# Half-array products of two heads issued in turn, and part of the mixer's VectorE work given to ScalarE, in a two-block transformer kernel on one core

## The chip, the cores and the metric

The kernel runs on one core of one Trainium2 chip. The metric is the device time of one execution in microseconds (us). The profiled execution is a single one, taken by the hardware profiler; its rows are what the prediction is worked out from.

The engines are named as in the profile: PE is TensorE's matrix product, PEld its weight load, DVE is VectorE, ACT is ScalarE, POOL is GpSimd, SP issues most DMAs.

## The reference

Two blocks follow each other on 512 tokens of width 1024 (batch 1). What matters here:

```python
# block 1: a mixer, then cross attention, then a mixture of 32 experts
def one_block(args):                                   # differential attention, 4 heads, 2 halves of 64
    s = jnp.einsum('bhmqd,bhmkd->bhmqk', q_blk, k)     # m = 0, 1: two halves of a head
    p = jax.nn.softmax(jnp.where(causal, s, -jnp.inf), axis=-1)
    a = p[:, :, 0] - lam * p[:, :, 1]
    return jnp.einsum('bhqk,bhkd->bhqd', a.astype(v.dtype), v)
...
qk = jax.nn.silu(causal_depthwise_conv(jnp.concatenate([mq, mk], axis=-1), ml_conv_w, ml_conv_b))  # 4 taps
...
# block 2, twice (two layers): a convolution beside an attention over selected keys
s_raw = jnp.einsum("bthd,bsd->bths", qi_b, k_idx_f)    # 8 index heads of 64
score = jnp.einsum("bth,bths->bts", w_b, jax.nn.relu(s_raw))
_, sel = lax.top_k(score, k_top)                       # 128 keys of each query
probs = jax.nn.softmax(...)                            # 8 heads, over the selected keys
o = jnp.einsum("bthk,btkc->bthc", probs, kv_sel)
o = jnp.einsum("bshc,hcd->bshd", o, w_uv)              # 64 output columns a head
```

The kernel multiplies the latent values by `w_uv` first, so that a head's last product has 64 output rows.

## The kernel before, in words

The program is one core's list of instructions. A scheduler orders them engine by engine, by priorities and its own estimate of times; each engine then works through its list in order. So an instruction that waits holds back what stands behind it on its engine.

Most products are made of float16 halves: a number is split into a high and a low part, and a product is three matrix products that add up in one PSUM bank (`mm3`, line 110: high by high, high by low, low by high; `mm`, line 99, issues each). `split` (lines 128 and 129) makes the parts, the high one on ACT, the low one on DVE. PSUM has eight banks; `bank(tag)` hands out those of a tag in turn. In the mixer `at` has three banks and `tr` two; in the layers of block 2 `at` has two, `tr` two and `po` one.

The changed places, in order of time:

- **Scores of the mixer's attention** (`diff_head`, lines 499 to 526). For each of 4 heads and 4 query blocks i the keys are W = 128 (i + 1) wide. Each half m of a head has 64 channels, so that its `mm3` fills 64 of the array's 128 rows, half 0 the upper and half 1 the lower ones. Then come a mask product (128 rows), on DVE the negated maximum (line 511) and its scaling (512), on ACT the exponential (514); when both halves are there, on DVE a reciprocal (517), a product with lambda (518), the scaling of half 1 (519) and the combination (520).
- **Convolution of the mixer** (`mlstm`, lines 594 to 606), 8 blocks of 128 channels: ACT copies the projection to `u` (595), DVE makes the first tap (597) and three more (600), ACT and DVE finish it. Its projections and those of the mixer's values are ordered between the attention's products.
- **Scores of the index heads** (`select`, line 1597), in each of two layers for query blocks i = 1, 2, 3: 8 heads of 64 channels, even heads in the upper and odd ones in the lower 64 rows. Each head's `mm3` goes to an `at` bank, ACT makes the positive part (1610) into one of two `re` buffers, DVE adds it up with the query's weight (1613, 1615), and then 16 rounds of a maximum and a replacement (1619, 1620) on DVE select the keys.
- **Values of the selected attention** (`dsa`, line 1625), four pairs of heads (hp) in each layer: softmax of a head, transposes by PE to `tr`, `split` into `pT`, and a `mm3` with 64 output rows into the upper (hh = 0) or lower (hh = 1) half of the one `po` bank, for key blocks k = 0 to 3 with 512, 384, 256 and 128 columns. The `pT{k}` have one buffer each.

The gates and the convolution's products of block 2 (`cv`, `mm`) stand between these in PE's list.

Of the kernel before, what the change touches and what calls it, by code (L numbers as in the profile page):

```python
# [12 lines left out]
F16 = mybir.dt.float16  # L13
BF16 = mybir.dt.bfloat16
I32 = mybir.dt.int32
AF = mybir.ActivationFunctionType
OP = mybir.AluOpType
AX = mybir.AxisListType
PSUM = bass.MemoryType.PSUM

P = 128
D = 1024
S = 512
NT = S // P
# [39 lines left out]
class Kern:  # L64
# [44 lines left out]
    def mm3(self, out, L, R, start, stop):  # L109
        self.mm(out, L[0], R[0], start, False)  # L110
        self.mm(out, L[0], R[1], False, False)
        return self.mm(out, L[1], R[0], False, stop)

# [377 lines left out]
    def diff_head(self, low, pool, qkh, qkl, vh, vl, lam, yy, h):  # L491
        nc = self.nc
        sc = 1.0 / (SA * SA * 8.0)
        if True:
# [4 lines left out]
            for i in range(NT):  # L499
# [3 lines left out]
                p = []  # L503
                for m in range(2):
                    rows = slice(m * 64, m * 64 + 64)
                    pS = self.bank("at")
                    qs = [t[rows, h, i * P:(i + 1) * P] for t in (qkh, qkl)]
                    ks = [t[rows, 4 + h, :W] for t in (qkh, qkl)]
                    self.mm3(pS[:, :W], qs, ks, True, False)
                    self.mm(pS[:, i * P:W], self.identb, self.mask_q, False, True)  # L510
                    nc.vector.tensor_reduce(nm[:, m:m + 1], pS[:, :W], AX.X, OP.max, negate=True)
                    nc.vector.tensor_scalar(nm[:, m:m + 1], nm[:, m:m + 1], sc, None, op0=OP.mult)
# [6 lines left out]
                nc.vector.tensor_scalar(p[1][:, :W], p[1][:, :W], sm[:, 1:2], None, op0=OP.mult)  # L519
# [30 lines left out]
    def mlstm(self, pool, xh, xl, qh, ql, gateb, yy):  # L550
# [37 lines left out]
        for k in range(4):  # L588
            w = self.load_w(a["w_pre"][6 + k])
            for bb in range(2):  # L590
# [6 lines left out]
                nc.vector.tensor_scalar(acc, u[:, 3:], convw[:, blk, 3:4], convb[:, blk:blk + 1],  # L597
                                        op0=OP.mult, op1=OP.add)
# [999 lines left out]
    def select(self, pool, i, qih, qil, kih, kil, widx):  # L1598
# [5 lines left out]
        for h in range(8):  # L1604
            rows = slice((h % 2) * 64, (h % 2) * 64 + 64)
            ps = self.bank("at")
            self.mm3(ps[:, :W], (qih[rows, h // 2, t], qil[rows, h // 2, t]),
                     (kih[rows, :W], kil[rows, :W]), True, True)
# [16 lines left out]
    def dsa(self, pool, ga, uq, cqh, cql, kvh, kvl, vh, vl, msk, yh, yl, hp):  # L1625
        nc, a = self.nc, self.a
        sc = 1.0 / (SA * SA * math.sqrt(128.0))
        po = self.bank("po")
        for hh in range(2):
# [26 lines left out]
            f = slice(h * 64, h * 64 + 64)  # L1656
            for k in range(NT):
                n = S - k * P
                pt = self.bank("tr")
                for i in range(k, NT):  # L1660
                    nc.tensor.transpose(pt[:, (i - k) * P:(i - k + 1) * P], ps_[i][:, k * P:(k + 1) * P],  # L1661
                                        self.ident)
                pT = pool.tile([P, 2, n], F16, name="pT", tag=f"pT{k}", bufs=1)
                self.split(pt[:, :n], pT[:, 0], pT[:, 1], 1024.0)
                self.mm3(po[hh * 64:hh * 64 + 64, k * P:], (vh[:, k, f], vl[:, k, f]), (pT[:, 0], pT[:, 1]),
                         k == 0, k == NT - 1)
# [276 lines left out]
```

## Time and profile before

| | |
|---|---|
| time, median of 3 runs | 1596.21 us (1591.71 to 1599.38) |
| profiled execution: its own time | 1596.56 us |
| profiled execution: span from the first to the last instruction | 1594.8 us |
| mean granted TensorE clock, as a share of full speed | 0.985 |
| PE busy | 1493.8 us, 94% of the span |
| DVE busy | 968.3 us, 61% |
| ACT busy | 591.7 us, 37% |
| POOL busy | 104.0 us, 7% |

A busy time is the union of an engine's instructions in the span. A PE product is recorded with the time that it takes to run through the array, so that products in a row overlap in the records; what one costs in a row is the distance between two starts. The profiled execution lies within the runs' range.

### The profile page before, as it was taken

How to read it: one execution, taken by the hardware profiler on the slowest of the kernel's cores; microseconds unless marked ns; L12 is line 12 of the kernel's file. 1: busy time of each engine (PE TensorE's matmuls, PEld its weight loads, DVE VectorE, ACT ScalarE, POOL GpSimd, SP SyncE). 2: the span in 40 equal slices, each digit the busy share in tenths (PEclk: the TensorE clock that was granted, in tenths of full speed). 3: DMA queues.
4: the chain of work that ended last, by engine and by line, in shares of the span. 5: the costliest groups of instructions: out<-in, count | busy, mean ns of one | idle time of the engine just before them, and what ended most of it. 6: DMA issues, size and time to landing. Idle time of an engine off the chain costs nothing.

```text
span 1594.8 us, 25367 instructions
## 1 busy us (share of the span) xinstructions
PE 1493.8 (94%) x10250; PEld 822.8 (52%) x10250; DVE 968.3 (61%) x2080; ACT 591.7 (37%) x1232; POOL 104.0 (7%) x120
## 2 busy tenths in 40 slices
PE   6899999899998999999999997898999989989998
PEld 5344586785585444444444434433544763335457
DVE  5768848888755234233243247897566668867553
ACT  5355545524532110111011016731567454227651
POOL 0210001100000000000000002211000012100000
PEclk9999999999999999999999999999999999899999
DMA  7420223589464999999999991334011222440101
GB/s 280 158 83 1 93 93 120 213 324 359 148 244 186 422 421 422 420 420 421 421 421 421 421 399 47 113 109 109 28 53 32 89 80 75 112 132 27 53 27 53
DMA packets 52984, 320.94 MB, mean 201 GB/s; under 512 B 6592, under 2 KB 9472, under 8 KB 16896
## 3 DMA queue, kind: packets, MB, share of 16 engines
q1 hardware_dynamic: 47440, 310.45, 50.0%
q10 hardware_dynamic: 5424, 8.85, 2.1%
q8 instruction: 81, 1.33, 0.3%
q14 instruction: 39, 0.32, 0.1%
HBM read 308.27 MB, written 3.69 MB: 196 GB/s over the span
## 4 chain that ended last, share of the span: by engine, by line
PE 46%; DVE 13%; ACT 4%; issue 3%; DMA 1%; POOL 1%; DVEq 0%; POOLq 0%; ACTq 0%
PE h L99 13%; PE y L99 7%; PE mm L99 6%; PE cv L99 5%; PE tr L99 4%; PE po L99 3%; PE ga L99 3%; PE at L99 3%; DVE sc L1620 2%; DVE m L1619 2%; DVE wl L129 2%; PE tr L1661 1%; DMA raw<-in_w_big 1%; PE tr L103 1%; ACT junk L190 1%
## 5 line engine op out<-in xcount | busy, mean ns | idle before, releaser
L99 PE MATMUL h<-raw,xg 128*64 128x512 f32 x1024 | 222.5, 592 | 0.2 <-DVE xg L938 0.2
L99 PEld LDWEIGHTS <-wh 128*128 128x128 f16 x1104 | 107.2, 99 | 131.0 <-issue 37.7
L129 DVE SCALAR_TENSOR_TENSOR wl<-raw,wh 128x1024 f16<-128x1024 f32 (+1 forms) x107 | 134.4, 1265 | 53.2 <-ACT wh L128 52.7
L99 PEld LDWEIGHTS h<-raw,xg 128*64 128x64 f32 x1024 | 73.4, 137 | 146.0 <-issue 141.9
L128 ACT ACTIVATE wh<-raw 128x1024 f16<-128x1024 f32 (+1 forms) x107 | 110.0, 1041 | 76.1 <-PE mm L99 35.8
L969 DVE SCALAR_TENSOR_TENSOR hm<-hm,h 128x512 f32<-128x512 f32 x16 | 11.0, 689 | 180.5 <-ACT hm L968 180.5
L99 PE MATMUL y<-raw,hT 128*64 128x512 f32 x512 | 113.6, 595 | 0.0
L998 DVE SCALAR_TENSOR_TENSOR x<-tr,x 128x512 f32<-128x512 f32 x128 | 86.3, 688 | 11.9 <-PE tr L99 9.8
L99 PEld LDWEIGHTS <-wl 128*128 128x128 f16 x552 | 54.9, 99 | 59.6 <-issue 10.9
L99 PE MATMUL cv<-hh,wh 128*128 128x512 f16 x192 | 75.3, 392 | 9.1 <-DVE ga L1356 9.1
L968 ACT ACTIVATE hm<-h 128x512 f32<-128x512 f32 x16 | 9.6, 597 | 197.8 <-PE h L99 182.8
L99 PEld LDWEIGHTS <-hh 128*128 128x128 f16 x768 | 72.8, 98 | 15.7 <-ACT hh L128 2.6
L129 DVE SCALAR_TENSOR_TENSOR yl<-y,cw,yh 128x512 f16<-128x512 f32 x32 | 24.0, 750 | 89.1 <-ACT yh L128 89.1
L99 PE MATMUL cv<-hh,wl 128*128 128x512 f16 x192 | 75.2, 392 | 0.0
L99 PE MATMUL cv<-hl,wh 128*128 128x512 f16 x192 | 75.2, 391 | 0.0
L99 PEld LDWEIGHTS y<-raw,hT 128*64 128x64 f32 x512 | 35.2, 137 | 70.3 <-issue 63.9
L99 PEld LDWEIGHTS <-hl 128*128 128x128 f16 x640 | 62.7, 98 | 14.6 <-issue 2.1
L99 PE MATMUL ga<-Sel,hl 128*128 128x128 f16 x480 | 65.8, 219 | 0.0
L99 PE MATMUL ga<-Sel,hh 128*128 128x128 f16 x480 | 65.7, 219 | 0.0
L128 ACT ACTIVATE yh<-y,cw 128x512 f16<-128x512 f32 x32 | 22.0, 687 | 114.2 <-PE y L99 112.9
L1263 DVE CUSTOM_DVE_ANT_0 raw<-raw,cact 128x1024 f32<-128x1024 f32 x48 | 58.3, 1238 | 4.5 <-DMA cact<-c_d 2.6
L161 POOL TENSOR_TENSOR rs_r<-rs_t,mhalf 128x1 f32<-128x1 f32 (+1 forms) x34 | 25.3, 748 | 485.2 <-DVE rs_t L160 485.2
(435 smaller groups left out, 3482.1 us busy)
## 6 DMA issues: line engine op xcount, KB each, us to landing
raw<-in_w_moe SPq DMA_DIRECT2D x192, 1024.0 KB, 19.8
raw<-in_w_pre SPq DMA_DIRECT2D x34, 1024.0 KB, 5.8
raw<-in_w_big SPq DMA_DIRECT2D x30, 1024.0 KB, 5.0
raw<-in_w_ada SPq DMA_DIRECT2D x24, 1024.0 KB, 5.2
R<-cu ACTq DMA_DIRECT2D x16, 271.0 KB, 5.4
R<-cu SPq DMA_DIRECT2D x16, 271.0 KB, 6.9
x<-in_x_tm SPq DMA_DIRECT2D x4, 512.0 KB, 8.9
out<-x SPq DMA_DIRECT2D x4, 512.0 KB, 2.6
```

The costliest lines, as they stand in the source:

```text
L99: self.last_mm = self.pin(self.nc.tensor.matmul(out, lhsT, rhs, start=start, stop=stop, skip_group_check=True))
L103: return self.pin(self.nc.tensor.transpose(out, src, ident))
L128: return (nc.scalar.activation(hi, src, func, scale=scale), nc.vector.scalar_tensor_tensor(lo, src, scale, hi, op0=OP.mult, op1=OP.subtract))
L129: nc.vector.scalar_tensor_tensor(lo, src, scale, hi, op0=OP.mult, op1=OP.subtract))
L161: self.last_pow = nc.gpsimd.tensor_tensor(r[:, :n], t[:, :n], self.mhalf[:, :n], OP.pow)
L190: self.nc.scalar.activation(junk[:, :src.shape[-1]], src, AF.Square, scale=scale, accum_out=out)
L969: nc.vector.scalar_tensor_tensor(hm[:n], hm[:n], 1.0, ph[0][:n], op0=OP.add, op1=OP.mult)
L998: self.last_add = nc.vector.scalar_tensor_tensor(xo, pc, 1.0 / 1024.0, xo, op0=OP.mult, op1=OP.add)
L1263: nc.vector.tensor_tensor_reduce(w, w, cact, 1.0, 0.0, OP.mult, OP.add, to)
L1619: nc.vector.max(m8, sc)
L1620: nc.vector.match_replace(sc, m8, sc, -3.0e38)
L1661: nc.tensor.transpose(pt[:, (i - k) * P:(i - k + 1) * P], ps_[i][:, k * P:(k + 1) * P], self.ident)
```

## The change

A new helper `mm3s` issues the three products of several outputs in turn: first high by high for each output, then high by low, then low by high, each made to stand behind the one before. It is used in three places: for the two halves of a head in `diff_head`, for an even and an odd head in `select`, and for the two heads of a pair in `dsa`. There the products of head hh = 0 now wait until head hh = 1 has its `pT` of the same key block, and the `pT` of hh = 1 go to the four buffers of tag `h`. In `diff_head` both masks stand behind the six products, and the two maxima are scaled by one DVE instruction. The scaling of half 1 (`pe`) and the first tap of the convolution (`acc`) go from DVE to ACT.

```diff
+    def mm3s(self, outs, Ls, Rs, start, stop):
+
+        prev = []
+        for n, (x, y) in enumerate(((0, 0), (0, 1), (1, 0))):
+            for out, L, R in zip(outs, Ls, Rs):
+                with self.after(*prev):
+                    prev = [self.mm(out, L[x], R[y], start and n == 0, stop and n == 2)]
+        return prev[0]
...
+                pSs = [self.bank("at") for _ in range(2)]
+                halves = [slice(r, r + 64) for r in (0, 64)]
+                last = self.mm3s([pS[:, :W] for pS in pSs],
+                                 [[t[r, h, i * P:(i + 1) * P] for t in (qkh, qkl)] for r in halves],
+                                 [[t[r, 4 + h, :W] for t in (qkh, qkl)] for r in halves], True, False)
                 for m in range(2):
...
-                    self.mm3(pS[:, :W], qs, ks, True, False)
-                    self.mm(pS[:, i * P:W], self.identb, self.mask_q, False, True)
-                    nc.vector.tensor_reduce(nm[:, m:m + 1], pS[:, :W], AX.X, OP.max, negate=True)
-                    nc.vector.tensor_scalar(nm[:, m:m + 1], nm[:, m:m + 1], sc, None, op0=OP.mult)
+                    with self.after(last):
+                        last = self.mm(pSs[m][:, i * P:W], self.identb, self.mask_q, False, True)
+                for m in range(2):
+                    nc.vector.tensor_reduce(nm[:, m:m + 1], pSs[m][:, :W], AX.X, OP.max, negate=True)
+                nc.vector.tensor_scalar(nm, nm, sc, None, op0=OP.mult)
...
-                nc.vector.tensor_scalar(p[1][:, :W], p[1][:, :W], sm[:, 1:2], None, op0=OP.mult)
+                nc.scalar.activation(p[1][:, :W], p[1][:, :W], AF.Copy, scale=sm[:, 1:2])
...
-                nc.vector.tensor_scalar(acc, u[:, 3:], convw[:, blk, 3:4], convb[:, blk:blk + 1],
-                                        op0=OP.mult, op1=OP.add)
+                nc.scalar.activation(acc, u[:, 3:], AF.Identity, scale=convw[:, blk, 3:4], bias=convb[:, blk:blk + 1])
...
-            rows = slice((h % 2) * 64, (h % 2) * 64 + 64)
-            ps = self.bank("at")
-            self.mm3(ps[:, :W], (qih[rows, h // 2, t], qil[rows, h // 2, t]),
-                     (kih[rows, :W], kil[rows, :W]), True, True)
+            if h % 2 == 0:
+                pss = [self.bank("at") for _ in range(2)]
+                halves = [slice(r, r + 64) for r in (0, 64)]
+                self.mm3s([p[:, :W] for p in pss], [(qih[r, h // 2, t], qil[r, h // 2, t]) for r in halves],
+                          [(kih[r, :W], kil[r, :W]) for r in halves], True, True)
+            ps = pss[h % 2]
...
-                pT = pool.tile([P, 2, n], F16, name="pT", tag=f"pT{k}", bufs=1)
+                pT = pool.tile([P, 2, n], F16, name="pT", **(dict(tag="h", bufs=BUFS["h"]) if hh else
+                                                             dict(tag=f"pT{k}", bufs=1)))
                 self.split(pt[:, :n], pT[:, 0], pT[:, 1], 1024.0)
-                self.mm3(po[hh * 64:hh * 64 + 64, k * P:], (vh[:, k, f], vl[:, k, f]), (pT[:, 0], pT[:, 1]),
-                         k == 0, k == NT - 1)
+                pTs.append(pT)
+                if hh:
+
+                    fs = [slice(g * 64, g * 64 + 64) for g in (h - 1, h)]
+                    self.mm3s([po[g * 64:g * 64 + 64, k * P:] for g in range(2)],
+                              [(vh[:, k, f], vl[:, k, f]) for f in fs],
+                              [(p[:, 0], p[:, 1]) for p in (pTs[k], pTs[NT + k])], k == 0, k == NT - 1)
```

How the scheduler now orders it is seen at three places. The first is PE's list in the mixer, at the first head's scores of query block i = 3, before (bank 934 is half 0; qkh and qkl are the high and low parts of queries and keys; weight loads are left out):

```order
L99 MATMUL at_934<-qkh_272 128x512
...
L99 MATMUL at_934<-qkl_273,qkh_272 128x512
...
L99 MATMUL at_934<-qkh_272,qkl_273 128x512
...
L99 MATMUL at_934<-mask_q_104,identb_103 128x128
L527 MATMUL tr_956<-ident_98,pe_869 128x128
```

The same place in the changed kernel, where bank 931 is half 0 and bank 932 half 1:

```order
L99 MATMUL at_931<-qkh_272 128x512
...
L99 MATMUL at_932<-qkh_272 128x512
...
L99 MATMUL at_931<-qkl_273,qkh_272 128x512
...
L99 MATMUL at_932<-qkl_273,qkh_272 128x512
...
L99 MATMUL at_931<-qkh_272,qkl_273 128x512
...
L99 MATMUL at_932<-qkh_272,qkl_273 128x512
...
L99 MATMUL at_931<-mask_q_104,identb_103 128x128
```

Half 0's first product stands alone, other products (left out) follow, and then the other five stand together, in turn, with the masks behind them. So it is for i = 1, 2 and 3; for i = 0 all six stand together.

The second place is PE's list at a pair's values, key block 0, in the first layer. Before (one head's `pT_11381`, with the gates' products `cv` between):

```order
L99 MATMUL po_11243<-pT_11381,v2_9901 64x512
L99 LDWEIGHTS wh_11423
L99 MATMUL cv_11457<-hl2_9295,wh_11423 128x512
L99 LDWEIGHTS wl_11424
L99 MATMUL cv_11457<-hh2_9294,wl_11424 128x512
...
L99 MATMUL cv_11457<-hh2_9294,wh_11423 128x512
L99 LDWEIGHTS v2_9901
...
L99 MATMUL po_11243<-pT_11391,v2_9901 64x384
```

After (`pT_11280` and `pT_11287` are the first head's, `pT_11353` and `pT_11366` the second's):

```order
L99 MATMUL po_11227<-pT_11353,v2_9885 64x512
L99 LDWEIGHTS v2_9885
L99 MATMUL po_11227<-pT_11280,v2_9885 64x512
L99 LDWEIGHTS wh_11403
L99 MATMUL cv_11441<-hh2_9278,wh_11403 128x512
...
L99 MATMUL cv_11441<-hl2_9279,wh_11403 128x512
...
L99 MATMUL cv_11441<-hh2_9278,wl_11404 128x512
...
L99 MATMUL po_11227<-pT_11287,v2_9885 64x384
...
L99 MATMUL po_11227<-pT_11366,v2_9885 64x384
```

The first head's first product has gone earlier (left out); the six of block 0 stand as one, two and three, those of block 1 join them without a break, six in turn, and blocks 2 and 3 repeat the pattern.

The third place is DVE's list in the mixer, at the second head's scores of query block i = 1. Before (nm holds the maxima, sm the sums, pe the exponentials, acc the convolution):

```order
L517 RECIPROCAL sm_1054<-sm_1054 128x2
L512 TENSOR_SCALAR nm_1077<-nm_1077 128x1 x2
L518 TENSOR_SCALAR sm_1054<-sm_1054,lam_851 128x1
L600 SCALAR_TENSOR_TENSOR acc_1632<-u_1629,mlc_244,acc_1632 128x512
L519 TENSOR_SCALAR pe_1071<-pe_1071,sm_1054 128x256
L511 TENSOR_REDUCE nm_1101<-at_1103 128x1
L520 SCALAR_TENSOR_TENSOR pe_1062<-pe_1062,sm_1054,pe_1071 128x256
```

After (line numbers are those of the changed kernel: 530 is the reciprocal, 522 the maximum, 523 its scaling, 533 the combination, 612 a tap, 138 the low part of a split):

```order
L530 RECIPROCAL sm_1049<-sm_1049 128x2
L138 SCALAR_TENSOR_TENSOR wl_1757<-raw_1750,wh_1756 128x1024
L531 TENSOR_SCALAR sm_1049<-sm_1049,lam_851 128x1
L522 TENSOR_REDUCE nm_1071<-at_1073 128x1
L522 TENSOR_REDUCE nm_1071<-at_1074 128x1
L533 SCALAR_TENSOR_TENSOR pe_1063<-pe_1063,sm_1049,pe_1065 128x256
L523 TENSOR_SCALAR nm_1071<-nm_1071 128x2
```

Both maxima of a pair now stand together, one scaling follows, and the combination comes without the scaling of half 1 ahead of it, which is in ACT's list.

## Rows read from the trace of the kernel before

**Rows 1.** The page: busy time by engine, and the chain's shares.

```profile
PE 1493.8 (94%) x10250; PEld 822.8 (52%) x10250; DVE 968.3 (61%) x2080; ACT 591.7 (37%) x1232; POOL 104.0 (7%) x120
...
PE 46%; DVE 13%; ACT 4%; issue 3%; DMA 1%; POOL 1%; DVEq 0%; POOLq 0%; ACTq 0%
```

**Rows 2.** Windows: stretch, us; busy PE, PEld, DVE, ACT, POOL; PEclk, DMA share, GB/s.

```profile
100.00:200.00 100.00, 92.58 (x564) 48.06 (x565) 86.84 (x228) 56.52 (x128) 5.91 (x4) 0.97 0.15 51
1035.00:1066.00 31.00, 29.16 (x203) 12.63 (x202) 31.00 (x93) 8.84 (x12) 3.94 (x4) 1.00 0.46 131
1066.00:1110.00 44.00, 38.06 (x225) 15.18 (x225) 40.37 (x77) 11.81 (x17) 5.06 (x6) 0.89 0.30 77
1145.00:1240.00 95.00, 93.25 (x493) 45.03 (x492) 62.81 (x141) 65.63 (x150) 0.00 (x0) 1.00 0.15 52
```

**Rows 3.** Groups of DVE instructions in 95 to 215 us, by shape.

```profile
L511 DVE TENSOR_REDUCE nm<-at 128x1 f32<-128x512 f32 x8 | 5.5, 689 | 3.2 <-PE at L99 3.0
...
L597 DVE TENSOR_SCALAR acc<-u,mlc 128x512 f32<-128x512 f32 x8 | 4.3, 539 | 0.3 <-ACT u L595 0.3
...
L512 DVE TENSOR_SCALAR nm<-nm 128x1 f32<-128x1 f32 x32 | 4.2, 144 | 0.0
...
L519 DVE TENSOR_SCALAR pe<-pe,sm 128x512 f32<-128x512 f32 x4 | 1.9, 480 | 0.0
...
L519 DVE TENSOR_SCALAR pe<-pe,sm 128x384 f32<-128x384 f32 x4 | 1.7, 413 | 0.0
L519 DVE TENSOR_SCALAR pe<-pe,sm 128x256 f32<-128x256 f32 x4 | 1.4, 346 | 0.0
...
L519 DVE TENSOR_SCALAR pe<-pe,sm 128x128 f32<-128x128 f32 x4 | 1.1, 278 | 0.0
```

**Rows 4.** Groups of ACT instructions in 95 to 215 us, by shape.

```profile
L514 ACT ACTIVATE pe<-at,nm 128x512 f32<-128x512 f32 x8 | 5.5, 685 | 5.1 <-DVE nm L512 5.1
...
L603 ACT ACTIVATE th<-acc 128x512 f32<-128x512 f32 x8 | 5.0, 628 | 5.9 <-DVE acc L600 4.5 <-DVE u L594 1.2
```

**Rows 5.** Timeline of DVE: start, duration, instruction.

```profile
174.79 0.34 DVE L519 TENSOR_SCALAR pe<-pe,sm 128x256 f32<-128x256 f32 x1
175.05 0.16 DVE L517 RECIPROCAL sm<-sm 128x2 f32<-128x2 f32 x1
```

**Rows 6.** Timeline of PE in the mixer's scores, half 1 of the first head.

```profile
105.29 0.38 PE L99 MATMUL at<-qkl,qkh 64*128 64x512 f16 x1
105.51 0.38 PE L99 MATMUL at<-qkh,qkl 64*128 64x512 f16 x1
105.82 0.23 PE L99 MATMUL at<-mask_q,identb 128*128 128x128 bf16 x1
```

**Rows 7.** Timeline of PE: runs of products in different parts of the array.

```profile
1021.79 0.51 PE L99 MATMUL at<-idx 64*128 64x256 f16 x6
...
1029.01 1.15 PE L99 MATMUL at<-idx 64*128 64x384 f16 x6
...
1116.15 5.36 PE L99 MATMUL po<-R,wd 128*32 128x512 f16 x96
```

**Rows 8.** Timeline of PE at a head's values, first layer.

```profile
1146.10 0.38 PE L99 MATMUL cv<-hh,wh 128*128 128x512 f16 x1
1146.42 0.39 PE L99 MATMUL po<-pT,v 128*64 128x512 f16 x1
1146.75 0.39 PE L99 MATMUL cv<-hl,wh 128*128 128x512 f16 x1
```

**Rows 9.** Waits of PE in 1145 to 1240 us: us, times, longest.

```profile
PE po L99 <- DVE pT L129: 0.9, 1, 0.9
```

**Rows 10.** Timeline of ACT and PE around the last index scores, first layer.

```profile
1073.28 0.60 ACT L1610 ACTIVATE re<-at 128x512 f32<-128x512 f32 x1 [1.60 <-PE at L99]
...
1108.18 0.58 PE L99 MATMUL cv<-hh,wh 128*128 128x512 f16 x1 [4.90 <-DVE ga L1356]
```

**Rows 11.** Instructions on the tile at: first and last start of the mixer's scores.

```profile
L99 PE MATMUL at<-qkh x32: 226/300/605, 96.5 to 174.1; 64*128 64x128 f16 x8, 64*128 64x256 f16 x8, 64*128 64x384 f16 x8, 64*128 64x512 f16 x8
```

More of the change, by code (lines that the diff above doesn't have):

```diff
@@ L503, in diff_head @@
                 p = []
-                for m in range(2):
[L505 to L508, printed above, removed]
-                    self.mm3(pS[:, :W], qs, ks, True, False)
-                    self.mm(pS[:, i * P:W], self.identb, self.mask_q, False, True)
-                    nc.vector.tensor_reduce(nm[:, m:m + 1], pS[:, :W], AX.X, OP.max, negate=True)
-                    nc.vector.tensor_scalar(nm[:, m:m + 1], nm[:, m:m + 1], sc, None, op0=OP.mult)
+                pSs = [self.bank("at") for _ in range(2)]
[3 more added lines that the diff above has]
+                                 [[t[r, 4 + h, :W] for t in (qkh, qkl)] for r in halves], True, False)
+                for m in range(2):
+                    with self.after(last):
[3 more added lines that the diff above has]
+                nc.vector.tensor_scalar(nm, nm, sc, None, op0=OP.mult)
+                for m in range(2):
+                    pS = pSs[m]
                     pe = pool.tile([P, W], F32, name="pe", tag=f"pe{i}", bufs=2) if m == 0 else self.t2(pool, "pe", "d")
@@ L1628, in dsa @@
         po = self.bank("po")
+        pTs = []
         for hh in range(2):
@@ L1655, in dsa @@
                 nc.scalar.activation(ps_[i], ps_[i], AF.Copy, scale=nm[:, 2, i:i + 1])
-            f = slice(h * 64, h * 64 + 64)
             for k in range(NT):
```

## The prediction

> **What bounds the kernel now.** I read the page first: PE is busy for 94% of the span, DVE for 61%, and PE has 46% of the chain that ended last against DVE's 13% [rows 1]. So a product saved is worth something only where PE is what the others wait for, and the change touches three stages with different limits. I therefore read windows of each stage [rows 2]. From 100 to 200 us, the mixer's attention and convolution, PE is busy for 92.6 us and DVE for 86.8 of 100: neither has much room, and ACT, with 56.5, has. From 1035 to 1066 us, the index scores and the rounds of selection, DVE is busy for 31.0 of 31 us, and from 1066 to 1110 for 40.4 of 44: DVE is the limit there, whatever PE does. From 1145 to 1240 us, the selected attention, PE is busy for 93.3 of 95 us, DVE for 62.8 and ACT for 65.6: PE is the limit. The second layer repeats both. The windows' other columns matter little, but PEclk is 0.89 in 1066 to 1110 us, which is a stretch at 1.2 instead of 2.4 GHz.
>
> **What the change saves on DVE in the mixer.** Three things go. Eight first taps at 539 ns make 4.3 us; sixteen scalings of half 1 at 480, 413, 346 and 278 ns, four of each, 6.1 us; sixteen of the 32 scalings of the maximum at 144 ns, 2.3 us [rows 3]. That is 12.7 us by durations, and I take the scaling of two columns to cost what one does. ACT gets eight taps, which I price by its tanh from one SBUF tile to another, 628 ns, so 5.0 us; and sixteen scalings, at most 685 ns, its 512-wide exponential, and by width about two thirds of that on average, 7 to 8 us [rows 4]. ACT then comes to some 69 of 100 us and can hold it. DVE's relief is less than the durations say: a scaling that starts at 174.79 and lasts 0.34 us is followed at 175.05, so that instructions overlap by 0.08 us in the records [rows 5]. Forty instructions fewer by 0.07 leave 10 us of relief.
>
> **What it saves on PE in the mixer.** A 512-wide product of a half costs 0.22 us in a row; going on to the mask, which fills the whole array, takes 0.31, so that a change of the part of the array in use costs about 0.1 us [rows 6]. Do products in different halves of the rows run at the same time? The trace of before has the answer: six 256-wide products of two index heads ended 0.51 us after the first began, where six 384-wide ones took 1.15 us [rows 7]. By width the six should have taken 0.8 us one by one; 0.51 is three passes. In columns it is the same: 96 products of 32 output columns each took 5.36 us, 0.056 us apiece against 0.22 for one that fills the array [rows 7]. So I count passes. For i = 0 six become three; for i = 1, 2, 3 the first stands alone and five make three passes, so six become four. Per head that saves three passes of 0.055 and two each of 0.11, 0.16 and 0.22 us, 1.1 us; four heads 4.5 us, and eight changes of the array's part 0.8 us. PE is relieved by 5.3 us, DVE by 10. Both were near full and the scheduler pulls later products into the stage, so I take 7 us, between the two. From below the bound is 0: the pair needs two of three `at` banks at once, and the first exponential now waits for the second maximum. From above it is 10.
>
> **What it saves in the values.** Before, a pair's key block makes six passes, 3.3 us over the four blocks at 0.22, 0.16, 0.11 and 0.055 us. After, blocks 1 and 3 make three, and 0 and 2, issued as one, two and three, make four: 2.0 us. Eight pairs in both layers save 10 us. Each group of values costs a change into and out of its part of the array: the steps from 1146.10 to 1146.42 and to 1146.75 are 0.32 and 0.33 us instead of 0.22 [rows 8]. Counted over PE's list, values stand in 76 groups before and 49 after, 54 changes less, 5.4 us. Together 15.6 us, 7.8 a layer, where PE waits for hardly anything now: its one wait on a `pT` is 0.9 us [rows 9]. I take 6 us a layer, 12 in all, because the first head's products no longer fill the time in which the second's softmax is made; ACT and DVE, with two thirds of the stage busy, would then be waited for. The bounds are 2 us a layer (two waits like the 0.9 us one in each pair, less what is saved) and 7.8. The `pT` of the second head have four buffers that nothing else uses in this stage; they cost nothing.
>
> The Trainium skill speaks against this on its page TensorEngine Tiling (Array Packing), section Performance Considerations: tiling speeds up TensorE but not the emptying of PSUM, which may then be the limit. The full DVE windows of the index scores agree; the values' window, with PE at 93 of 95, does not. By that rule all but the mixer's gain would go; it is the third rival below.
>
> **What it does in the index scores.** Little. PE's list gets ten groups more, 2 us dearer over both layers. Passes fall, but runs of three and three already ran side by side where both banks were free [rows 7]. DVE sets the pace: PE waited 4.9 us for DVE's gates at the stage's end, so products saved before that are given back [rows 10]. What can hurt is the pair's hold on both banks: five products can start only when the second bank is read, and then ACT waits for them, as it did for 1.60 us where PE was slow [rows 10]. A pair loses some 0.35 us so (three passes of 0.22 and the array's depth, less the time in which DVE still has a buffer), and of twelve pairs a layer perhaps two or three have no cover. I take a loss of 1 us; the bounds are a gain of 3 (the slow stretch costs less with fewer passes) and a loss of 8 (0.35 us for each of 24 pairs).
>
> The Trainium skill, on TensorE: Matmul & The Clock Gate, Part 3, has matmuls start and end strictly in program order. By it a run of three and three makes five passes, and the change would save PE some 3 us a layer here (one or two passes of 0.16 us in each of twelve pairs, an estimate). The 0.51 us run is three and three in the program and took three passes, so the trace disagrees, and I count nothing.
>
> **The sum.** 7 and 12, less 1, is 18 us off. The profiled execution took 1596.56 us and the median is 1596.21, so they can be used alike: 1578.6, **1579 us**. What the mixer gains passes on: the experts are started by the routing that hangs on it.
>
> **Rivals.**
> 1. The mixer gains nothing: ACT's new work and the pair's two banks lengthen the path from product to product as much as the relief shortens it. For it speaks that ACT waited 5.1 us for the scaled maximum of the 512-wide scores alone [rows 4], and this now comes later. Against it, DVE's list is shorter. 1579 + 7 = 1586.
> 2. All that is saved passes on: 10 from the mixer, 15.6 from the values, 3 from the index scores: 1568.
> 3. The values gain nothing, as softmax and `split` set their pace, and the index scores lose their bound: 1596.6 - 7 + 8 gives 1598, without that loss 1590. I take 1591. Against it: PE waits for `pT` once.
> 4. **Slower:** the mixer's pairs become a chain through two banks. From the second bank's release on, a 512-wide pair needs three passes (0.65 us), a change and two masks (0.2), two maxima of 0.69 [rows 3], a scaling (0.14) and an exponential of 0.69 [rows 4] before the next pair's second bank is free: 3.1 us, by width some 2 on average, 32 for 16 pairs. The scores are now made from 96.5 to 174.1 us [rows 11], so 46 us are left for queueing, 0.7 us at each of the four handoffs of a pair. If engines this busy let each wait longer, every 0.1 us costs 6.4; at 1.1 us it is 26 us more, the gain of 7 is gone, and the time is 1579 + 7 + 26 = 1612. It is slower than before from 0.9 us on. Against it: the scheduler put other products between the first and the other five, and the order of heads is kept.
>
> **How the numbers follow.** Chances: forecast 0.58 (own range 1571 to 1587), rival one 0.16, two 0.08, three 0.10, four 0.08. A measurement of this kernel tells a difference of about 0.5%, 8 us, from none: faster is below 1588. The forecast gives 0.56 to faster and 0.02 to the same, rival one 0.11 and 0.05, two 0.08, three 0.02 and 0.08, four 0.08 to slower: 0.77, 0.15 and 0.08. The range goes from rival two's gain with a little more, 1564, to 1594; it leaves out rival four and the ends of two and three.
>
> **What would show it.** In the profile after, the values' products should start in pairs some 0.01 us apart, and 1145 to 1240 us should be shorter by about 6 us with PE's share of its time lower; a new wait of PE for DVE's `pT` of several us would mean rival three. In the mixer DVE's busy time should fall by some 10 us, and the mixer's end come 7 us earlier; if PE waits for ACT's `pe` at the `at` banks instead, it is rival one or four. The rounds of selection should take as long as before. What would make me wrong apart from these: a longer or shorter stretch at 1.2 GHz, since the scheduler's new order moves the pauses before which PE's clock falls.

## The result, and the profile after

The changed kernel took 1576.85 us in the median of 4 runs (1575.46 to 1584.72), the kernel before 1597.15 us in 4 runs beside them: a ratio of 0.9895, 95% interval 0.9861 to 0.9929. A second set of six runs gave 1578.37 us and 0.9915 (0.9882 to 0.9948). The profiled execution took 1575.46 us with a span of 1573.8, 21.0 us less than the span before. The prediction was 1579 us.

The page of the changed kernel, busy times and the chain's shares, which answer to [rows 1]:

```profile
PE 1467.4 (93%) x10240; PEld 814.1 (52%) x10250; DVE 963.0 (61%) x2040; ACT 604.4 (38%) x1256; POOL 103.6 (7%) x120
...
PE 48%; DVE 11%; ACT 4%; issue 3%; POOL 1%; DMA 1%; DVEq 0%; POOLq 0%; ACTq 0%
```

PE lost 26 us of busy time, DVE 5.3 us and 40 instructions; ACT gained 13 us and 24 instructions.

Windows of the same stages, which come 4 us earlier from the index scores on; they answer to [rows 2]:

```profile
100.00:200.00 100.00, 92.43 (x645) 52.60 (x643) 87.53 (x199) 75.27 (x162) 5.86 (x5) 1.00 0.18 64
1031.00:1062.00 31.00, 29.03 (x202) 12.11 (x201) 31.00 (x89) 10.09 (x15) 3.89 (x4) 1.00 0.44 123
1062.00:1106.00 44.00, 37.29 (x229) 14.99 (x229) 41.64 (x84) 11.59 (x17) 5.10 (x7) 0.90 0.31 80
1141.00:1232.00 91.00, 85.84 (x495) 43.01 (x497) 62.79 (x143) 66.14 (x153) 0.00 (x0) 1.00 0.15 53
```

The last row is the selected attention: PE is now busy for 94% of it instead of 98%, and it is 4 to 5 us shorter with the same work of DVE and ACT. In the mixer the same 100 us hold 81 more of PE's products; in the selection DVE is still busy for 31.0 of 31 us.

DVE's and ACT's groups in 95 to 215 us, which answer to [rows 3, 4]:

```profile
L523 DVE TENSOR_SCALAR nm<-nm 128x2 f32<-128x2 f32 x16 | 2.6, 161 | 0.1
```

```profile
L610 ACT ACTIVATE acc<-u,mlc 128x512 f32<-128x512 f32 x8 | 6.4, 806 | 0.1
...
L532 ACT ACTIVATE pe<-pe,sm 128x512 f32<-128x512 f32 x4 | 2.9, 716 | 0.0
```

Two columns scaled at once cost 161 ns, one cost 144. On ACT a tap takes 806 ns, where the prediction had 628, and a 512-wide scaling 716, where it had at most 685.

PE's timeline at a pair's values, which answers to [rows 8]:

```profile
1154.82 0.41 PE L99 MATMUL po<-pT,v 128*64 128x512 f16 x2
...
1157.33 1.11 PE L99 MATMUL po<-pT,v 128*64 128x512 f16 x9
1158.37 0.44 PE L1675 MATMUL tr<-ident,lg 128*128 128x128 f32 x2
1158.73 0.30 PE L99 MATMUL po<-pT,v 128*64 128x256 f16 x1
```

Two 512-wide products end 0.41 us after the first began, where one alone takes 0.39 [rows 8]: they ran at the same time. Their starts lie 3 ns apart; over both layers 57 of the 96 possible pairs start within 0.03 us of each other, none before. Nine take 1.11 us. The single one at 1158.73 is the product that the scheduler pulls ahead.

PE's waits in the selected attention: total, times, longest. The first fence is before (1145 to 1240 us, beside [rows 9]), the second after (1141 to 1232 us).

```profile
PE at L99 <- DVE nm L1648: 0.3, 1, 0.3
```

```profile
PE at L99 <- DVE nm L1663: 2.8, 4, 1.3
```

And in the mixer (95 to 215 us), before and after:

```profile
PE tr L527 <- DVE pe L520: 1.3, 2, 0.7
```

```profile
PE tr L540 <- DVE pe L533: 4.9, 5, 2.3
...
PE at L99 <- ACT pe L527: 0.3, 1, 0.3
```

In the first stage PE now waits at the next pair's scores for the maxima of the softmax; the wait for DVE's `pT` is gone. In the second it waits longer for DVE's combination, which stands behind the scaling that moved to ACT. The wait for ACT's `pe` at the `at` banks, which was to be the sign of rivals one and four, is 0.3 us; before it was 1.5.

**Where the time went, by stage.** A stage here runs from the first product of one kind to the first of the next (mixer: up to the experts' first product; then the experts; index 1 and 2: first index score to the last product of the convolution; values 1: from there to the next layer's first index score; values 2: to the end). The table gives each profile's length against the kernel before, and in brackets how many us of the stage had a granted clock of half, 1.2 GHz. The kernels are those of the experiments below.

```
kernel           mixer          experts        index 1        values 1       index 2        values 2, end
before           497.1 (10.2)   518.0 ( 0.0)   112.4 (13.7)   194.0 ( 6.8)   112.7 (13.7)   160.7 ( 3.3)
after             -5.2 (13.7)    +0.9 ( 3.4)    +0.0 (13.7)    -5.2 ( 6.8)    -5.7 ( 3.4)    -5.8 ( 2.2)
joined_again      -4.2 (17.1)    +0.2 ( 0.0)    -1.5 (10.2)    -5.0 ( 6.8)    -2.9 ( 3.4)    -5.8 ( 4.9)
values_alone      +6.5 (23.9)    -0.1 ( 0.0)    -2.0 ( 6.8)    -5.0 ( 6.8)    -1.6 (13.7)    -5.8 ( 2.3)
scores_alone      -7.0 ( 6.8)    -0.1 ( 0.0)    -0.0 (13.7)    -0.1 ( 6.8)    +0.6 (13.7)    +0.1 ( 4.1)
act_alone         -8.0 ( 6.8)    +0.1 ( 0.0)    +3.6 (20.5)    -0.1 ( 6.8)    -1.6 (13.7)    +0.2 ( 5.0)
index_alone       +8.9 (27.3)    +0.1 ( 0.0)    -0.7 (10.2)    -0.1 ( 6.8)    -3.6 ( 3.4)    +0.1 ( 3.0)
no_act            -5.9 (13.7)    -0.2 ( 0.0)    -2.3 ( 6.8)    -4.0 (10.2)    -3.7 ( 6.8)    -4.3 ( 5.7)
scaling_back      -7.5 ( 6.8)    +0.6 ( 3.4)    -0.5 (13.7)    -5.1 ( 6.8)    -2.1 (10.2)    -5.8 ( 5.4)
values_row       -10.6 ( 3.4)    +1.0 ( 3.4)    -0.8 (13.7)    -2.1 ( 6.8)    -5.0 ( 6.8)    -2.3 ( 2.2)
values_first      -4.4 ( 6.8)    +0.7 ( 3.4)    -0.1 (13.7)    -5.9 ( 6.8)    -1.5 ( 6.8)    -6.7 ( 4.6)
all_first         -3.5 (17.1)    +0.3 ( 0.0)    -3.4 ( 6.8)    -6.9 ( 3.4)    -1.8 (10.2)    -8.9 ( 3.2)
no_index          -5.9 (13.7)    +0.2 ( 0.0)    +1.8 (20.5)    -5.0 ( 6.8)    -1.3 (13.7)    -5.5 ( 3.1)
first_no_index    -7.0 ( 6.8)    +0.1 ( 0.0)    +2.1 (20.5)    -6.1 ( 6.8)    -4.7 ( 6.8)    -6.5 ( 4.9)
```

Read the values' columns first: the kernels whose values are joined in turn stand at -4.0 to -6.9 and -4.3 to -8.9, values_row at -2.1 and -2.3, and those whose values are as before within 0.2 of 0. The mixer's column is noisier for a reason that can be read off it: values_alone and index_alone have the instructions of the kernel before in that stage, in the same order, and are 6.5 and 8.9 us longer, with 13.7 and 17.1 us more at 1.2 GHz. So about half of the time at the lower clock is lost there, and a mixer is compared after taking off half of its bracket: before 492.0, after 6.9 us less, joined_again 7.6 less. So taken, the others with a changed mixer lie 5.3 to 7.6 us below before; values_first, with 2.7, falls out. Its mixer has the changed kernel's instructions in the same order, and 3 us of the difference arise between 304 and 336 us, behind all that the change touches; why is not shown.

**What PE spent on the three kinds of products.** Summed over each trace: from the start of each product to the start of PE's next one (a step over 0.45 us, which holds a wait, counts with the product's width alone), and what the step into a group takes beyond its own product's width, in us:

```
kernel           values            mixer's scores    index scores
before           35.1 + 7.4        16.9 + 3.4        27.7 + 3.4
after            21.4 + 4.8        11.4 + 2.7        20.6 + 3.7
values_row       28.4 + 6.6        11.4 + 2.7        21.1 + 4.0
values_first     17.1 + 3.1        11.6 + 2.8        21.2 + 3.9
no_index         21.5 + 5.1        11.4 + 2.7        28.2 + 3.5
```

### The profile page after: what moved, and what is told of

The parts are those of the page before. It is cut to its first block, busy times and chain, and to the rows that moved or that the text cites. A ratio compares the mean times of both kernels' runs of the same rounds, so it can differ in the third digit from the quotient of the medians.

```text
span 1573.8 us, 25337 instructions
## 1 busy us (share of the span) xinstructions
PE 1467.4 (93%) x10240; PEld 814.1 (52%) x10250; DVE 963.0 (61%) x2040; ACT 604.4 (38%) x1256; POOL 103.6 (7%) x120
## 4 chain that ended last, share of the span: by engine, by line
PE 48%; DVE 11%; ACT 4%; issue 3%; POOL 1%; DMA 1%; DVEq 0%; POOLq 0%; ACTq 0%
PE h L99 13%; PE mm L99 7%; PE y L99 7%; PE cv L99 6%; PE tr L99 4%; PE ga L99 3%; PE po L99 3%; PE at L99 2%; DVE wl L138 2%; DVE sc L1634 2%; DVE m L1633 1%; PE tr L1675 1%; PE tr L103 1%; DVE sc L1629 1%; ACT junk L199 1%
## 5 line engine op out<-in xcount | busy, mean ns | idle before, releaser
L1010 DVE SCALAR_TENSOR_TENSOR x<-tr,x 128x512 f32<-128x512 f32 x128 | 86.4, 687 | 12.5 <-PE tr L99 10.5
```

Source lines behind the costliest of these rows:

```text
L1010: self.last_add = nc.vector.scalar_tensor_tensor(xo, pc, 1.0 / 1024.0, xo, op0=OP.mult, op1=OP.add)
```

## The experiments

"Joined" stands for products that are issued in turn by `mm3s`. The first four kernels do one part each on the kernel before, 11 or 12 runs each on one chip. Every ratio is to runs of the kernel before on the same chip.

**Only the values joined** (the change of `dsa` alone).

```diff
+                    self.mm3s([po[g * 64:g * 64 + 64, k * P:] for g in range(2)], ...
```

> Only the values of the selected attention are joined. If PE sets the pace of that stage, as the prediction has it, this alone gives about 11 us (the trace of the change shows some 5 and 6 us in the two layers), so 1586 us. If softmax and the splits set the pace (rival three), within 3 us of before, 1593 to 1599. A third theory, that the gain of the changed kernel comes mostly from where stretches at 1.2 GHz fall, would give any time from 1585 to 1600 and show it in the clock column, not in the windows of the values.

1588.26 us, ratio 0.9938 (0.9914 to 0.9962): 9.9 us off in the timed runs, and 5.0 and 5.8 us off the two stages in the profile. PE sets the pace there; rival three falls.

**Only the mixer's scores joined**, with one scaling of both maxima.

```diff
+                last = self.mm3s([pS[:, :W] for pS in pSs], ...
+                nc.vector.tensor_scalar(nm, nm, sc, None, op0=OP.mult)
```

> Only the mixer's scores are joined, with one scaling of both maxima; half 1's scaling and the first tap stay on DVE. If saved passes on PE carry the mixer's gain, 4 to 5 us less, 1592. If DVE's relief carries it, or both are needed since both engines were near full, 0 to 2 us less, 1594 to 1596. If the pair's hold on two banks costs something that the moves to ACT only cover up (rival four, small), 1598 to 1606.

1589.46 us, ratio 0.9965 (0.9947 to 0.9983): 5.6 us off.

**Only the moves to ACT.**

```diff
-                nc.vector.tensor_scalar(p[1][:, :W], p[1][:, :W], sm[:, 1:2], None, op0=OP.mult)
+                nc.scalar.activation(p[1][:, :W], p[1][:, :W], AF.Copy, scale=sm[:, 1:2])
-                nc.vector.tensor_scalar(acc, u[:, 3:], convw[:, blk, 3:4], convb[:, blk:blk + 1],
-                                        op0=OP.mult, op1=OP.add)
+                nc.scalar.activation(acc, u[:, 3:], AF.Identity, scale=convw[:, blk, 3:4], bias=convb[:, blk:blk + 1])
```

> Only half 1's scaling and the convolution's first tap go from DVE to ACT; all products stay as they were. If DVE's relief carries the mixer's gain, 4 to 5 us less, 1592. If the saved passes on PE carry it, or both are needed, 0 to 2 us less. If a softmax that now goes from DVE to ACT and back is longer than it was, up to 5 us more.

1590.75 us, ratio 0.9969 (0.9953 to 0.9985): 4.9 us off. Each part of the mixer alone gives what either theory had for the one that carries the gain.

**Only the index scores joined.**

```diff
+                self.mm3s([p[:, :W] for p in pss], [(qih[r, h // 2, t], qil[r, h // 2, t]) for r in halves], ...
```

> Only the index scores are joined. The prediction has DVE as the limit there and a loss of 1 us: 1595 to 1598. In the trace of the changed kernel the second layer's index scores and convolution are some 6 us shorter, the first layer's as long as before. If that is a real gain of the saved passes, both layers should show it here or the second alone, 1588 to 1591; if it is where a stretch at 1.2 GHz falls, the time is 1595 to 1598 with such a stretch of 10 us or more in the second layer as before, and moves with it.

1593.87 us, ratio 0.9985 (0.9970 to 1.0000): 2.4 us off. The second layer's stage is 3.6 us shorter with 3.4 us at 1.2 GHz instead of 13.7; the first layer's is 0.7 shorter. The time is between the two theories.

The next four are the changed kernel once more and with one part changed back, on another chip.

**The changed kernel again.**

> The changed kernel once more, for a narrower interval and a second profile. The four parts done alone gave 9.9, 5.6, 4.9 and 2.4 us off, 22.8 together; the changed kernel's own median gave 20. If the parts add up, 1573 to 1577. If the two parts in the mixer share one gain (the profile of the change has the mixer only 5 us earlier, those of the parts alone have it 7 and 8 us earlier), 1577 to 1581. In its profile, stretches at 1.2 GHz before the experts and in the second layer's index scores should differ from the first profile's, if they are chance from one execution to the next; if they belong to the order of the instructions, they stand where they stood, within a microsecond.

1578.37 us, ratio 0.9915 (0.9882 to 0.9948). The parts alone add up to 22.8 us; the whole gave 20 and 14 in the medians of its two sets, 17 and 14 by the ratios. The medians do not settle whether they add up; the table at the end of this section does. Stretches at 1.2 GHz stood where they had stood, within 1 us, at 62, 209, 243, 1062, 1103 and 1294 us; others came and went (964, 1015 and 1401 us in the first profile, 417 and 1366 in the second). So the order of instructions sets most of them, and chance some.

**The moves to ACT taken back.**

```diff
-                nc.scalar.activation(p[1][:, :W], p[1][:, :W], AF.Copy, scale=sm[:, 1:2])
+                nc.vector.tensor_scalar(p[1][:, :W], p[1][:, :W], sm[:, 1:2], None, op0=OP.mult)
...
-                nc.scalar.activation(acc, u[:, 3:], AF.Identity, scale=convw[:, blk, 3:4], bias=convb[:, blk:blk + 1])
```

> The changed kernel with half 1's scaling and the first tap back on DVE; all three groups of products stay joined. If the moves to ACT add their 4.9 us to the rest, this is 5 us slower than the changed kernel. If both parts of the mixer share one gain, it is 0 to 2 us slower. If the moves put ACT on the path of the attention's transposes, it is up to 3 us faster.

1575.68 us, ratio 0.9897 (0.9867 to 0.9927): not slower than the changed kernel, and 2.7 us faster in the median. With the scores joined, the moves to ACT are worth nothing that can be measured. PE's waits in 95 to 215 us of this kernel's profile:

```profile
PE tr L540 <- DVE pe L533: 3.2, 5, 1.0
```

The wait for the combination is 3.2 us instead of 4.9.

**Half 1's scaling alone back on DVE.**

```diff
-                nc.scalar.activation(p[1][:, :W], p[1][:, :W], AF.Copy, scale=sm[:, 1:2])
+                nc.vector.tensor_scalar(p[1][:, :W], p[1][:, :W], sm[:, 1:2], None, op0=OP.mult)
```

> The changed kernel with half 1's scaling back on DVE; the first tap stays on ACT. The new wait of PE in the mixer is for the combination that follows this scaling, 4.9 us in five waits. If the way from DVE to ACT and back causes it, this is 2 to 4 us faster than the changed kernel; if the relief of DVE by 16 scalings (about 5 us) is worth more, 2 to 4 us slower; if neither is on the path, within 1 us of it.

1576.20 us, ratio 0.9896 (0.9867 to 0.9925), inside the intervals of the two runs before. PE's wait for the combination is 3.2 us here too, so it is the scaling's way over ACT that makes it 4.9; but where the scaling stands makes no difference in time that can be told here.

**The values in a row instead of in turn.**

```diff
-        for n, (x, y) in enumerate(((0, 0), (0, 1), (1, 0))):
-            for out, L, R in zip(outs, Ls, Rs):
+        for out, L, R in zip(outs, Ls, Rs):
+            for n, (x, y) in enumerate(((0, 0), (0, 1), (1, 0))):
```

> The changed kernel, but the values' products of a key block stand in a row, three of the first head and then three of the second, instead of in turn; the groups are 64 instead of 49 (76 before). The prediction counts two savings here, 10 us of passes and 5.4 us for fewer changes of the array's part. If products in different column halves start only in the order of the program, a block takes five or six passes: 7 to 9 us slower than the changed kernel, that is nearly the time without the joined values. If three and three run side by side as those of the index scores did in the kernel before, only the 15 groups more are lost: 1 to 3 us slower. If the gain came from fewer changes alone, also 3 us, but without products that start in pairs in the profile.

1583.25 us, ratio 0.9940 (0.9916 to 0.9964), and only 2.1 and 2.3 us left in the stages. The profile says why. Its timeline of PE at a pair's values:

```profile
1151.23 1.11 PE L99 MATMUL po<-pT,v 128*64 128x512 f16 x8
1152.27 0.44 PE L1684 MATMUL tr<-ident,lg 128*128 128x128 f32 x2
1152.64 0.52 PE L99 MATMUL po<-pT,v 128*64 128x256 f16 x3
```

The eight stand in the program as two 512-wide of the second head, three 384-wide of the first and three of the second. Their starts, read from the same trace:

```
1151.234 512   1151.241 384   1151.427 384   1151.474 512
1151.590 384   1151.690 384   1151.852 384   1152.015 384
```

A 384-wide product of the first head starts 7 ns after the first 512-wide one and before the second, which the program has ahead of it. Each half ran its own products one behind the other, and the halves beside each other: the second head's five make 0.24 + 0.22 + 3 x 0.16 = 0.94 us, and 0.1 for the change of part gives the 1.04 us up to the transpose. What is lost is elsewhere. The first head's three no longer wait for the second's, so the scheduler issues them earlier, as the three at 1152.64, and nothing is left to run beside the second's. Neither expectation had that.

The last four are meant to show how much is left; the first three of them share one chip, the last ran on another. In **the second head's product first**, no product can be issued before both heads have their `pT`.

```diff
-                    fs = [slice(g * 64, g * 64 + 64) for g in (h - 1, h)]
-                    self.mm3s([po[g * 64:g * 64 + 64, k * P:] for g in range(2)],
+                    fs = [slice(g * 64, g * 64 + 64) for g in (h, h - 1)]
+                    self.mm3s([po[g * 64:g * 64 + 64, k * P:] for g in (1, 0)],
...
-                              [(p[:, 0], p[:, 1]) for p in (pTs[k], pTs[NT + k])], k == 0, k == NT - 1)
+                              [(p[:, 0], p[:, 1]) for p in (pTs[NT + k], pTs[k])], k == 0, k == NT - 1)
```

> The changed kernel, but in the values the second head's product stands first of each two. Nothing of a block can then be issued before the second head's splits, so no single product is pulled ahead: the groups in PE's list are 33 instead of 49, and blocks 0 and 2 make three passes instead of four. By the sum's own rates that is 16 groups times two changes of 0.1 us, 3.2 us, and 16 passes of 0.16 us on average, 2.6 us: 5 to 6 us faster than the changed kernel, if PE still sets the pace of the stage. If softmax and splits set it by now (the values gave 4.9 us a layer where 7.8 were worked out), within 2 us of the changed kernel, with waits of PE for pT in the profile.

1577.20 us, ratio 0.9873 (0.9849 to 0.9898). PE spends 6.0 us less on the values (17.1 + 3.1 for 21.4 + 4.8), as worked out, but the two stages are only 0.7 to 0.9 us shorter each. PE's timeline and, in 1127 to 1235 us, its longer waits:

```profile
1155.13 0.41 PE L99 MATMUL po<-pT,v 128*64 128x512 f16 x2
1157.65 1.11 PE L99 MATMUL po<-pT,v 128*64 128x512 f16 x10
```

```profile
PE at L99 <- DVE nm L1663: 3.0, 4, 1.3
PE mm L99 <- DVE ga L1771: 1.2, 1, 1.2
```

Ten take as long as nine or eight did. PE no longer sets the pace alone: it waits for the softmax's maxima, and at the end 1.2 us for the gated output, 0.2 in the changed kernel.

**The second half's product first in all three places.**

```diff
-                last = self.mm3s([pS[:, :W] for pS in pSs],
+                last = self.mm3s([pS[:, :W] for pS in pSs[::-1]],
...
-                self.mm3s([p[:, :W] for p in pss], ...
+                self.mm3s([p[:, :W] for p in pss[::-1]], ...
```

> As the run before, and in the mixer's scores and in the index scores too the product into the second bank stands first, so that six stand together. By passes and changes on PE alone this saves a further 3 to 4 us. If the single early product was worth something, since the rest waits for the second bank anyway and DVE or ACT set the pace there, it is the same as the run before within 2 us, or slower by 1 to 4 us, with longer waits of ACT and DVE for PE at the index scores.

1572.01 us, ratio 0.9840 (0.9817 to 0.9864): the lowest median of all, though the interval overlaps that of the next kernel. The time fell by 5.2 us more, in the way of the first theory but not for its reason. In the trace one product still stands ahead of the other five in most pairs; there are 30 groups in the mixer's scores and 46 in the index scores, as many as in the changed kernel, and PE spends the same time on them within 0.1 us. The first product does not stand behind the later bank: in the program's list the first product of a pair, now that of the other half, takes the bank that comes free first. For the index scores this is bank 4 and bank 5 by turns from pair to pair, where it is always 4 in the changed kernel. So no pass was saved there. The stage table puts the further gain into index 1 and the values, with less time at 1.2 GHz in each of the first layer's; the mixer, less half of its bracket, is 7.0 us below before, as in the changed kernel (6.9). What made this kernel faster is not shown.

**The changed kernel without the joined index scores.**

```diff
-                self.mm3s([p[:, :W] for p in pss], ...
+            self.mm3(ps[:, :W], (qih[rows, h // 2, t], qil[rows, h // 2, t]),
```

> The changed kernel without the joined index scores. Done alone they gave 2.4 us where the prediction had a loss of 1. In all five profiles with them the second layer's index stage has 3.4 to 10.2 us at 1.2 GHz, in all four without them 13.6 or 13.7; a shorter such stretch is worth up to half of the difference, 2 to 5 us. If that is the gain, this run is 2 to 5 us slower than the changed kernel and has 13 us at 1.2 GHz there. If it is chance, it is within 1 us, or the stretch is short here too.

1574.02 us, ratio 0.9856 (0.9829 to 0.9883), 0.4 and 0.6% below the changed kernel's two ratios, where both theories had it as fast or slower, though its profile has the 13.7 us at 1.2 GHz in the second layer. The six runs go from 1570.4 to 1580.9 us, the lower the clock the longer: 0.989 and 0.990 in the three shortest.

**The second half's product first, index scores as before.**

> The second bank's product first in the mixer's scores and in the values, as in the run before the last, but the index scores one head after the other as in the kernel before. Joining the index scores saves PE some 7 us of product time over both layers in every profile that has it, yet done alone it gave 2.4 us and left out of the changed kernel it cost nothing. If DVE's rounds take that saving back, as the prediction has it, this is within 2 us of the version with all three (1572). If the shorter stretches at 1.2 GHz in the second layer are worth something, 2 to 5 us slower, 1574 to 1577. If holding two banks for a pair costs, 2 to 5 us faster, 1567 to 1570.

1578.72 us, ratio 0.9894 (0.9877 to 0.9911): 6.7 us slower in the median than with all three, 8.6 by the ratios, more than any theory had. The last two kernels contradict each other on the index scores.

**All timed runs at one clock.** Much of the scatter among a kernel's runs goes with the mean granted clock. Take the 166 timed runs of this section, 69 of them of the kernel before, and fit one level for each kernel, one for each chip and one slope for all: each 0.001 of the mean clock goes with 1.21 us (0.12) less time, and 1.8 us of scatter are left. Brackets hold two standard errors. At the same clock the kernels are faster than the kernel before by, in us:

```
values_alone  10.5 (1.3)   scores_alone  5.3 (1.2)   act_alone     4.9 (1.2)   index_alone    -0.7 (1.3)
joined_again  14.3 (1.8)   no_act       15.2 (1.8)   scaling_back 13.2 (1.8)   values_row      8.0 (1.7)
values_first  16.3 (1.9)   all_first    20.5 (1.9)   no_index     17.0 (1.9)   first_no_index 16.4 (1.9)
```

Three things can be read from it. The parts come to 20.0 us (3.3) and the whole, joined_again, to 14.3, so they do not add up: 5.7 us (3.8) are missing, about what one of the mixer's two parts gives alone. The index scores joined alone gain nothing; their 2.4 us came with a mean clock of 0.986 instead of 0.984. In the changed kernel joining them costs 2.7 us (2.6), with the second half first it gains 4.1 (2.6): no sign holds. And the values in a row give back 6.4 us (2.0), as the stages do (6.6). What a kernel's order of instructions does to the clock itself is taken off here and cannot be read from this table.

## Why the prediction was right, point by point

**The values: right in mechanism and nearly in size.** The term was 12 us. PE's time for them fell from 42.5 to 26.2 us, 16.3 where 15.6 were worked out; 10.8 us of it arrived in the profile with the values joined alone, 9.9 in its timed runs, 10.5 at one clock. The share that was left off, for a first head whose products no longer cover the second's softmax, was a little larger: PE waits 2.8 us for `nm` in that stretch, 0.3 before. The lower bound of 2 us a layer does not come out of its own terms: 7.8 less two waits of 0.9 us in each of four pairs is 0.6. Nothing in the sum rests on it. Past this point the share falls: of the next 6.0 us on PE, values_first got 1.6. The rival by the Trainium skill's TensorEngine Tiling (Array Packing), Performance Considerations, with the emptying of PSUM as the limit, did not hold in this stage.

**The mixer: right in size, wrong in how it was put together.** The term was 7 us; with half of the time at 1.2 GHz taken off, the changed kernel's mixer is 6.9 and 7.6 us shorter. PE's relief was 6.2 us (20.3 to 14.1) for 5.3. DVE's was not 10: its durations before the experts fall from 416.0 to 404.1 us, nearly the 12.7 worked out, but its busy time on the page by only 5.3 (968.3 to 963.0). So 6.6 us of overlap went with the 40 instructions, 0.17 us each, where the prediction took 0.07 from a single pair [rows 5]. The other step that fails is to place the gain between the two reliefs, as if both were needed: joined scores alone shorten the mixer by 5.3 us, the moves alone by 6.3 (7.0 and 8.0 in the table, less half of the 3.4 us by which their brackets are smaller). Either gives most of what both give, and taken back from the whole the moves cost nothing. PE's wait for the combination is 1.3 us before, 3.2 or 3.3 with the scores joined and 4.9 with the scaling moved as well; that it is the reason was not shown, and the kernel without the last 1.7 us of it, scaling_back, gained nothing that can be told. Rivals one and four fall.

**The index scores: right that little comes of it, wrong count of passes.** The term was a loss of 1 us, with nothing for saved passes, since runs of three and three already ran side by side where both banks were free. They did at 1021.79 us [rows 7], but in the trace before only 12 of the 72 possible pairs of products start within 0.03 us of each other, 53 after. PE's time for them fell from 31.1 to 24.3 us, about 3.4 us a layer. The Trainium skill, TensorE: Matmul & The Clock Gate, Part 3, gave 3 us a layer as worked out ahead; in that size the trace agrees, but not in its reason, an order of starts that is strictly the program's, which the eight starts above do not keep.

The saving lies under DVE's rounds as long as PE runs at 2.4 GHz. Where it doesn't, PE is the limit. The second layer's index stage before and after (window, length; busy PE, PEld, DVE, ACT, POOL; PEclk, DMA share, GB/s):

```profile
1369.00:1377.00 8.00, 5.69 (x18) 1.48 (x17) 8.00 (x23) 1.84 (x4) 2.55 (x4) 0.76 0.52 139
1377.00:1387.00 10.00, 10.00 (x24) 2.71 (x23) 5.80 (x15) 2.23 (x4) 0.00 (x0) 0.51 0.00 2
```

```profile
1358.00:1366.00 8.00, 5.66 (x30) 2.00 (x25) 8.00 (x25) 1.92 (x4) 3.94 (x4) 1.00 0.70 232
1366.00:1376.00 10.00, 9.93 (x76) 4.14 (x79) 9.97 (x24) 3.21 (x6) 0.00 (x0) 1.00 0.00 0
```

Before, the clock fell in a stretch in which PE paused, and in the next ten us PE was always busy and DVE for 5.8 us only; after, PE paused as much, the clock stayed, and DVE was busy for 9.97. Over all profiles, the eight with joined index scores have 11.1 and 6.4 us at 1.2 GHz in the two layers' stages on average and the six without 16.0 and 12.5; the stages are 2.1 and 1.9 us shorter. That would be a gain of 4 us, near the bound of 3 that the prediction gave for just this, but half of the 11 us less at 1.2 GHz would alone make 5.5. By the ratios of the timed runs joining gains 2.4 us alone, gains 8.6 with the second half's product first, and loses 6 to 9 in the changed kernel; at one clock these are -0.7, 4.1 and -2.7, about nothing, and the forecast loss of 1 us is not refuted. What stays open is whether the joined scores cause the shorter stretches.

**The sum** was 18; the two sets gave 20 and 14 in the medians, and the second gave 14.3 (1.8) at one clock. The first set's four runs, brought to the clock of the kernel before by the same slope, come to 1580 us. So that the first median, 1576.85, lies below the forecast is luck of the clock, and at one clock the sum is some 4 us too large. The terms as measured, 10.8 and 6.9 less 0.7 to 2.7, make 15 to 17. How far the clock moves a run is seen in the 69 runs of the kernel before made beside the experiments: the mean granted clock goes from 0.980 (1598.8 to 1604.1 us) to 0.991 (1582.4 us), and the time with it. Of the 21 us between the first two profiles 5.7 fell in index 2, with 10.3 us less at 1.2 GHz.

## What to carry to other kernels

Count what a packed product saves in the stage where PE has the last wait: there two thirds of PE's saving became time, under a busy DVE little that could be measured. Two products in different halves of the array run together only if both are ready when they are issued; a chain that alternates them and begins with the one that is ready last kept the scheduler from pulling some ahead to run alone, in the values, where the operand was late. It did not in the scores, where a bank was late and the first product took the first free bank. When two engines are both nearly full, relieve one and measure before relieving the other. And before a difference under 0.5% is read as the change's own, set the runs side by side at the same clock.

## What the runs showed of the hardware

Products in one half of the array's columns started ahead of products that the program has before them in the other half: a 384-wide one 7 ns after the first of two 512-wide ones, 0.23 us before the second. An ACT tap with a scale and a bias per partition took 806 ns, its tanh of the same size 628 [rows 4]. And the same instructions in the same order, up to the experts, took 8.9 us more in one profile than in another, with 17.1 us more at 1.2 GHz; over the 166 timed runs 0.001 of the mean granted clock went with 1.21 us.
